# Giving out the product of the attention weights with V two items behind the logits instead of one

## The chip, the cores and the metric

The kernel runs on one core of one Trainium2 chip, in one launch. The metric is device time in microseconds (us); lower is better. Beside the time of each run there is one execution taken by the hardware profiler, from which all rows below come. PE is TensorE (matrix products), PEld its weight loads, DVE is VectorE, ACT ScalarE, POOL GpSimd, SP SyncE.

## The reference, cut to what matters

Everything is fp32. A sequence of 512 tokens of width 1024 passes a first block with three branches (a "fox" attention with forget gates and 12 heads of 64, an S5 state space, a memory attention with 4 heads of 128 over 256 memory rows), then two layers of a second block (attention A with 8 query heads on 2 key heads; attention B with three dilated groups of 4 heads; a wide MLP).

```python
# first block
h = rms_norm(x, g_norm); z = h @ w_in        # q, k, v, forget gates, S5 input, memory q, gates
s = q @ k.T / 8 + F[:, None] - F[None, :]    # fox: F is the cumulated log forget gate, causal
y_fox = softmax(s) @ v * silu(gf)
y_s5 = gelu(s5_ssm(u, ...)); y_s5 = y_s5 * sigmoid(y_s5 @ w_glu + b_glu) * silu(gs)
y_mem = softmax(qm @ mk.T / sqrt(128)) @ mv * silu(gm)
merged = g0 * (y_fox @ w_proj_fox) + g1 * (y_s5 @ w_proj_s5) + g2 * (y_mem @ w_proj_mem)
x = rms_norm(x + merged @ w_out, g_final)
# second block, for each of two layers
h = rms(x, g_mix) * (1 + sc1) + sh1; parts = h @ w_in
y_a = softmax(rope(qa) @ rope(ka).T / 8) @ va @ w_branch_a
y_b = dilated_attention(rope(qs), rope(ks), vs) @ w_branch_b
x = x + gt1 * ((sigmoid(ga) * y_a + sigmoid(gb) * y_b) @ w_out)
x = x + gt2 * (relu(h2 @ w_ff1) ** 2 @ w_ff2)
```

## The kernel before, in words

Each fp32 product is made as three products of rounded halves: a matrix is cast to its high part (`wh`, `ph`, `yh`), the rest is its low part (`wl`, `pl`, `yl`), and PE adds high·high, high·low and low·high in one PSUM tile (lines 117 to 119 and 133 to 135 for the layers' weights). For each strip of weights ACT casts the high part (line 93), and DVE or POOL subtracts it to give the low part (line 96).

All four kinds of attention go through `Att.unit`. There are 16 units: six of fox (two heads each), two of memory, and in each of the two layers two of attention A and two of attention B. A unit has two lists of items. The first list finds each query row's maximum: `s_item` makes logits and reduces them (line 345), and at its end `m_item` splits all maxima in three bf16 parts on DVE (`split3`, lines 267 to 271) and turns them with four products on PE (`turn`, line 277; the split maxima are named mcm, or mcq in attention B). The second list goes over the heads and, within a head, over blocks of keys, 168 items in all (48 of fox, 8 of memory, 56 in each layer). `t_item` makes the logits with keys on the partitions (line 320), ACT takes the exponential (pe, line 388) and rounds it (ph, line 390), DVE subtracts to get pl (line 392). `pv_item` adds the three products with V into the head's PSUM tile ppv (lines 409 to 411: V high·ph, V low·ph, V high·pl). After a head's last one `out_item` copies the sums out (lines 436 and 437), and after a pair's last, in fox, DVE takes the reciprocal (line 439) and POOL multiplies (line 440).

PSUM has three tiles for layer products ("mm"), four in one ring for logits, sums, turns and S5 ("s"), and one for the products with V ("pv").

Items of one unit's second list are dealt among those of the next unit's first list by their relative place (`mix`), and that list among items of projections by counting (`merge`). Each item ends with a tick, which pays the background generators: the S5 batches advance at 0.2, later 0.25, of the ticks during fox and memory. A batch makes s5bt and its product (lines 1259, 1268), copies it (s5b, line 1308), multiplies by weights s5cw (line 1312), copies again (s5to, line 1317) and makes the outputs (lines 1321 to 1323).

None of this is the final order. The program's text gives each instruction a place, and the framework's scheduler then puts the instructions of each engine in an order of its own; buffers, semaphores and waits follow from it. So a shift at one place can reorder every engine anywhere behind it. DVE copies and the normalisation of a row (lines 190, 197, 210, "nr") stand in the same queues.

Of the kernel before, what the change touches and what calls it, by code (L numbers as in the profile page):

```python
# [234 lines left out]
class Att(Core):  # L235

    @staticmethod
    def cut(t, c):  # L240
# [50 lines left out]
    def unit(self, nh, sregs, tregs, qk, vsl, dst, extra=None, nq=4, hd=64, orow=None, fold=None):  # L291
# [82 lines left out]
        def t_item(j, i):  # L374
            if i == 0:
                st["pv", j] = self.p("pv")
            regs, pvs = tregs()[i]
            lo_c = min(c0 for c0, *_ in regs)
            pt = self.p("s")
            w = slice(lo_c, max(c0 + n for c0, n, *_ in regs))  # L380
            qs = w if isinstance(regs[0][3], slice) else regs[0][3]
            own = extra is None and fold is None
            if own:
                nc.tensor.matmul(self.like(pt[:, w], qs), self.selm[j], self.cut(st["mr"], qs), start=True, stop=False)
            for r_i, reg in enumerate(regs):
                region_mm(pt, j, reg, not own and r_i == 0, r_i == len(regs) - 1, True)
            e = self.u(name="pe")
            nc.scalar.activation(out=e[:, w], in_=pt[:, w], func=AF.Exp)  # L388
            ph = self.u(F32R, "ph")
            nc.scalar.copy(ph[:, w], e[:, w])  # L390
            pl = self.u(F32R, "pl")
            nc.vector.tensor_tensor(out=pl[:, w], in0=e[:, w], in1=f32(ph)[:, w], op=ALU.subtract)  # L392
            st["p", j, i] = (ph, pl, pvs)
# [3 lines left out]
        def pv_item(j, i):  # L397
            ph, pl, pvs = st.pop(("p", j, i))
            pv = st["pv", j]
            mm = nc.tensor.matmul  # L400
            for x, (g, kb, c) in enumerate(pvs):
                vh, vl = vsl(j, g, kb)
                o = c
                f = i == 0 and x == 0
                z = i == nt - 1 and x == len(pvs) - 1
                if not isinstance(c, slice):
                    o = slice(0, 4 * (c[1] - c[0]))
                h, lo = self.like(ph[:, o], c), self.like(pl[:, o], c)
                mm(self.cut(pv, c), vh, h, start=f, stop=False)  # L409
                mm(self.cut(pv, c), vl, h, start=False, stop=False)  # L410
                mm(self.cut(pv, c), vh, lo, start=False, stop=z)  # L411
            if i == nt - 1:
                out_item(j)
# [8 lines left out]
        def out_item(j):  # L422
            pv = st.pop(("pv", j))
            v = vrow(j)
            if own_sum:
                rb = self.u(name="rb")
                pb = self.p("m")
                nc.tensor.matmul(pb, self.selr1[j], st["mr"], start=True, stop=True)
                nc.scalar.copy(rb, pb)
                nc.vector.tensor_tensor(out=dst(j), in0=pv, in1=rb, op=ALU.mult)  # L430
                return
            if j % 2 == 0:
                st["rs"] = self.u(name="rs")
            rows = slice(64 * (j % 2), 64 * (j % 2) + 64)
            rs, y = st["rs"], dst(j)
            nc.scalar.copy(rs[rows], pv[64 - v.start:128 - v.start])
            nc.scalar.copy(y[rows], pv[v])
            if j % 2 == 1:
                nc.vector.reciprocal(out=rs, in_=rs)
                nc.gpsimd.tensor_tensor(out=y, in0=y, in1=rs, op=ALU.mult)  # L440
# [3 lines left out]
        seq = [(j, i) for j in range(nh) for i in range(nt)]  # L444
        t = []
        for k, (j, i) in enumerate(seq):
            def it(j=j, i=i, k=k):
                t_item(j, i)
                if k > 0:
                    pv_item(*seq[k - 1])  # L450
            t.append(it)
        t.append(lambda: pv_item(*seq[-1]))
        t = [(lambda f=f: (f(), self.tick(1.0))) for f in t]
        s = [(lambda f=f: (f(), self.tick(0.5))) for f in s]
        return s, t
# [1598 lines left out]
```

## Time and profile before

| | us |
|---|---|
| median of three runs | 2462.0 |
| fastest and slowest of them | 2461.26 and 2466.11 |
| the profiled execution | 2459.34 |
| its span, first to last instruction | 2457.6 |

The profiled execution is 2.7 us under the median and has 1.7 us around its span. The mean clock that was granted to TensorE is 0.981 of full speed in it. Rows give start and duration in us from the span's start; the bracket at a row's end is the time the engine idled before it, and what ended that.

### The profile page before, as it was taken

What the parts mean: (1) busy time and instruction counts of PE and PEld (TensorE: products, weight loads), DVE (VectorE), ACT (ScalarE), POOL (GpSimd) and SP (SyncE); (2) the same over time, 40 slices, a digit from 0 to 9 for tenths busy, and PEclk for the clock granted to TensorE, in tenths of its full rate; (3) what the DMA queues carried; (4) which work ended last, traced back from release to release, by engine and by line L of the source; (5) the groups of instructions that cost most, each with busy time, mean ns of one, the idle gap of its engine ahead of it and who ended that gap; (6) DMA issues with size and microseconds to landing.
All of it is one profiled execution on the core that took longest, in us unless ns stands there. A gap on an engine that the chain in (4) does not pass through costs nothing.

```text
span 2457.6 us, 33152 instructions
## 1 busy us (share of the span) xinstructions
PE 2322.2 (94%) x12138; PEld 1938.8 (79%) x12138; DVE 1538.6 (63%) x2573; ACT 1064.0 (43%) x1995; POOL 887.5 (36%) x810
## 2 busy tenths in 40 slices
PE   6999989989999889998999999998999899999999
PEld 5877768877888767787888888897778788888888
DVE  7567787657899788658278674257874746422222
ACT  4345543443333336643444324343565344533422
POOL 2445446635222264225132223126531523123212
PEclk9999999999999999999999999998999999999999
DMA  4311123312676321122137563232212224223222
GB/s 158 104 44 52 56 75 101 112 43 84 233 270 226 124 83 43 60 77 79 61 129 259 201 217 120 77 138 73 77 36 69 77 69 138 71 101 112 89 92 86
DMA packets 105620, 265.37 MB, mean 108 GB/s; under 512 B 13664, under 2 KB 23408, under 8 KB 105456
## 3 DMA queue, kind: packets, MB, share of 16 engines
q1 hardware_dynamic: 104304, 261.47, 31.5%
q8 instruction: 96, 1.57, 0.3%
q10 hardware_dynamic: 1152, 1.77, 0.2%
q14 instruction: 68, 0.56, 0.1%
HBM read 244.69 MB, written 9.44 MB: 103 GB/s over the span
## 4 chain that ended last, share of the span: by engine, by line
PE 63%; DVE 11%; issue 4%; ACT 3%; POOL 2%; DMA 1%; SPq 1%; DVEq 0%; POOLq 0%; ACTq 0%
PE pmm L117 17%; PE pmm L118 17%; PE pmm L119 17%; PE ps L320 3%; DVE wl L96 1%; DVE adacc L514 1%; DMA xs<-xg 1%; PE ppv L411 1%; PE ppv L410 1%; PE ppv L409 1%; DVE l L232 1%; PE pmm L134 1%; PE pmm L135 1%; PE pmm L133 1%; DVE xs L636 1%
## 5 line engine op out<-in xcount | busy, mean ns | idle before, releaser
L96 POOL TENSOR_TENSOR wl<-wr,wh 128x512 fp32r<-128x512 f32 x346 | 480.8, 1409 | 1122.6 <-ACT wh L93 968.0
L117 PE MATMUL pmm<-h,wh 128*128 128x512 f32 (+1 forms) x2112 | 824.1, 391 | 5.7 <-ACT wh L93 3.2
L119 PE MATMUL pmm<-h,wl 128*128 128x512 f32 (+1 forms) x2112 | 821.2, 389 | 2.1 <-POOL wl L96 1.8
L118 PE MATMUL pmm<-l,wh 128*128 128x512 f32 (+1 forms) x2112 | 819.5, 388 | 0.0
L119 PEld LDWEIGHTS pmm<-h,wl 128*128 128x128 f32 x2112 | 399.1, 189 | 85.7 <-POOL wl L96 4.3
L117 PEld LDWEIGHTS pmm<-h,wh 128*128 128x128 f32 x2112 | 399.4, 189 | 84.7 <-ACT wh L93 4.7
L118 PEld LDWEIGHTS pmm<-l,wh 128*128 128x128 f32 x2112 | 399.6, 189 | 77.3 <-DVE l L230 0.4
L93 ACT CAST wh<-wr 128x512 fp32r<-128x512 f32 (+1 forms) x692 | 385.1, 610 | 136.8 <-DMA wr<-in_w 118.8
L96 DVE TENSOR_TENSOR wl<-wr,wh 128x512 fp32r<-128x512 f32 x346 | 278.8, 836 | 30.3 <-ACT wh L93 26.9
L392 DVE TENSOR_TENSOR pl<-pe,ph 128x512 fp32r<-128x512 f32 (+4 forms) x168 | 121.4, 731 | 149.8 <-ACT ph L390 144.7
L230 DVE TENSOR_TENSOR l<-r,h 128x512 fp32r<-128x512 f32 x64 | 46.5, 726 | 220.9 <-ACT h L222 216.8
L971 DVE SCALAR_TENSOR_TENSOR x<-pmm,ada,x 128x512 f32<-128x512 f32 (+1 forms) x88 | 59.9, 682 | 180.5 <-PE pmm L119 180.0
L320 PE MATMUL ps<-qk,qk 128*128 128x512 f32 (+4 forms) x416 | 142.9, 381 | 24.6 <-POOL qk L683 7.4
L514 DVE SCALAR_TENSOR_TENSOR adacc<-adw,cact,adacc 128x512 f32<-128x512 f32 x168 | 156.5, 932 | 3.2
L994 ACT ACTIVATE r<-pmm 128x512 f32<-128x512 f32 x62 | 37.1, 598 | 257.1 <-PE pmm L119 257.1
L388 ACT ACTIVATE pe<-ps 128x512 f32<-128x512 f32 (+4 forms) x168 | 84.6, 503 | 102.8 <-PE ps L320 102.4
L320 PEld LDWEIGHTS ps<-qk,qk 128*128 128x128 f32 x416 | 81.0, 199 | 51.7 <-POOL qk L683 13.3
L117 PE MATMUL pmm<-yh,wh 128*128 128x512 f32 (+1 forms) x244 | 91.2, 377 | 5.8 <-ACT yh L1419 3.7
L632 POOL TENSOR_TENSOR qv<-qv,mhalf 128x8 f32<-128x8 f32 x34 | 62.9, 1852 | 86.6 <-DVE qv L631 83.1
L119 PE MATMUL pmm<-yh,wl 128*128 128x512 f32 (+1 forms) x244 | 90.7, 373 | 1.7 <-DVE wl L96 0.9
L390 ACT CAST ph<-pe 128x512 fp32r<-128x512 f32 (+4 forms) x168 | 88.8, 529 | 7.8 <-PE ppv L410 1.5
L118 PE MATMUL pmm<-yl,wh 128*128 128x512 f32 (+1 forms) x244 | 90.6, 372 | 0.3 <-DVE yl L1089 0.3
(386 smaller groups left out, 3993.2 us busy)
## 6 DMA issues: line engine op xcount, KB each, us to landing
wr<-in_w SPq DMA_DIRECT2D x324, 512.0 KB
adw<-in_wada SPq DMA_DIRECT2D x192, 256.0 KB
xs<-xg SPq DMA_DIRECT2D x136, 64.0 KB
wr<-in_w SPq DMA_DIRECT2D x22, 384.0 KB
xd<-x SPq DMA_DIRECT2D x16, 256.0 KB
x<-xd SPq DMA_DIRECT2D x16, 256.0 KB
x<-in_x SPq DMA_DIRECT2D x16, 128.0 KB
x<-in_x SPq DMA_DIRECT2D x8, 256.0 KB
```

Of the source, the lines that this page charges most:

```text
L93: ins = self.nc.scalar.copy(h[:, 0:m], r[:, c:c + m])
L96: eng.tensor_tensor(out=l[:, 0:m], in0=r[:, c:c + m], in1=f32(h)[:, 0:m], op=ALU.subtract)
L117: mm(out, wh, ah, start=start, stop=False)
L118: mm(out, wh, al, start=False, stop=False)
L119: self.pe = mm(out, wl, ah, start=False, stop=stop).ins.name
L320: mm(outs[i] if len(r.shape) == 2 else outs[i].rearrange("p (r i) -> p r i", r=r.shape[1]), w, r, start=first and i == 0, stop=last and i ...
L388: nc.scalar.activation(out=e[:, w], in_=pt[:, w], func=AF.Exp)
L390: nc.scalar.copy(ph[:, w], e[:, w])
L392: nc.vector.tensor_tensor(out=pl[:, w], in0=e[:, w], in1=f32(ph)[:, w], op=ALU.subtract)
L514: nc.vector.scalar_tensor_tensor(out=acc, in0=w, scalar=cc, in1=acc, op0=ALU.mult, op1=ALU.add)
L632: nc.gpsimd.tensor_tensor(out=v, in0=v, in1=self.mhalf, op=ALU.pow)
L971: nc.vector.scalar_tensor_tensor(out=x[j][:, s], in0=pm[:, s], scalar=ada[:, c + j:c + j + 1], in1=x[j][:, s], op0=ALU.mult, op1=ALU.add)
```

## The change

Within a unit, the products with V of item k-2 follow the logits of item k, where those of item k-1 did. The last two products of a unit become items of their own, where one did. So a unit's second list has one entry more (and pays one tick more), and the relative places that `mix` and the counts that `merge` deal by shift with its length. No instruction's arithmetic is altered, and each engine has the same work. Lines behind the new one are numbered one higher after the change.

```diff
@@ class Att(Core) @@
+    LAG = 2
@@ def unit(...) @@
         for k, (j, i) in enumerate(seq):
             def it(j=j, i=i, k=k):
                 t_item(j, i)
-                if k > 0:
-                    pv_item(*seq[k - 1])
+                if k >= self.LAG:
+                    pv_item(*seq[k - self.LAG])
             t.append(it)
-        t.append(lambda: pv_item(*seq[-1]))
+        t += [(lambda v=v: pv_item(*v)) for v in seq[len(seq) - self.LAG:]]
         t = [(lambda f=f: (f(), self.tick(1.0))) for f in t]
```

What the built programs' queues show, at three places.

VectorE in layer 0, where the second list of the first attention A unit (pl) and the first list of the next (unm, the reduced maxima) run beside the rotary embedding of the projections to come (xg, xs, rope). Before:

```order
L345 TENSOR_REDUCE unm_2012_8992<-ps_2019_9007 128x1
L345 TENSOR_REDUCE unm_2012_8992<-ps_2024_9022 128x1
L345 TENSOR_REDUCE unm_2012_8992<-ps_2025_9025 128x1
L392 TENSOR_TENSOR pl_2018_9005<-pe_2016_9001,ph_2017_9003 128x512
L647 TENSOR_TENSOR xg_1952_8725<-xg_1952_8725,ps_2032_9063 128x512
L392 TENSOR_TENSOR pl_2023_9017<-pe_2021_9013,ph_2022_9015 128x512
L636 TENSOR_TENSOR xs_2010_8984<-xs_2010_8984,rope_1814_7987 128x512
```

and after:

```order
L346 TENSOR_REDUCE unm_2012_8992<-ps_2019_9007 128x1
L346 TENSOR_REDUCE unm_2012_8992<-ps_2024_9019 128x1
L393 TENSOR_TENSOR pl_2018_9005<-pe_2016_9001,ph_2017_9003 128x512
L346 TENSOR_REDUCE unm_2012_8992<-ps_2029_9034 128x1
L637 TENSOR_TENSOR xs_2010_8984<-xs_2010_8984,rope_1814_7987 128x512
L648 TENSOR_TENSOR xg_1952_8725<-xg_1952_8725,ps_2036_9072 128x512
L393 TENSOR_TENSOR pl_2023_9017<-pe_2021_9013,ph_2022_9015 128x512
```

The second pl stood ahead of xs and now stands behind xs and xg.

VectorE at the turn of the fifth fox unit's maxima: the CASTs and subtractions of mcm0 and sp3 are the split in three, on which PE's turn waits; qk belongs to a projection, s5to to an S5 batch, wl to layer weights. Before:

```order
L345 TENSOR_REDUCE unm_550_2548<-ps_599_2722 128x1
L96 TENSOR_TENSOR wl_586_2656<-wr_475_2154,wh_585_2655 128x512
L345 TENSOR_REDUCE unm_550_2548<-ps_600_2727 128x1
L670 SCALAR_TENSOR_TENSOR qk_589_2686<-pmm_588_2661,qk_589_2686 64x512
L267 CAST mcm0_6_74<-unm_550_2548 128x4x4
L268 TENSOR_TENSOR sp3_605_2746<-unm_550_2548,mcm0_6_74 128x16
L269 CAST mcm0_6_74<-sp3_605_2746 128x4x4
L325 MEMSET unm_1092_4897 128x16
L270 TENSOR_TENSOR sp3_605_2746<-sp3_605_2746,mcm0_6_74 128x16
L1086 TENSOR_TENSOR s5cw_577_2641<-s5w_579_2643,s5w_580_2644 64x16x16
L670 SCALAR_TENSOR_TENSOR qk_590_2689<-pmm_588_2661,qk_590_2689 64x512
```

and after (four s5to copies, of which three are shown):

```order
L346 TENSOR_REDUCE unm_554_2560<-ps_607_2759 128x1
L393 TENSOR_TENSOR pl_604_2750<-pe_602_2746,ph_603_2748 128x384
L268 CAST mcm0_6_74<-unm_554_2560 128x4x4
L269 TENSOR_TENSOR sp3_612_2778<-unm_554_2560,mcm0_6_74 128x16
L1318 COPY s5to_599_2730<-ps_598_2721 32x512
...
L1318 COPY s5to_599_2730<-ps_598_2721 32x4x64
L1318 COPY s5to_599_2730<-ps_598_2721 32x4x32
L270 CAST mcm0_6_74<-sp3_612_2778 128x4x4
L326 MEMSET unm_1096_4909 128x16
L393 TENSOR_TENSOR pl_611_2773<-pe_609_2769,ph_610_2771 128x256
L271 TENSOR_TENSOR sp3_612_2778<-sp3_612_2778,mcm0_6_74 128x16
L272 CAST mcm0_6_74<-sp3_612_2778 128x4x4
```

Four copies of the S5 batch now stand between the first steps of the split. On PE, between the unit's last logits for maxima and this turn, stood 31 products, 24 of them of layer weights, and now stand 20, none of layer weights.

PE at the end of the last fox unit: ppv is the head's sum, pmm with h, l, wh and wl a projection, L1312 and L1321 to L1323 an S5 batch (one line higher after), L190 and L197 a normalisation, and yh the gated result going into the next projection. Before:

```order
L409 MATMUL ppv_768_3445<-ph_809_3601,v_482_2217 128x128
L410 MATMUL ppv_768_3445<-ph_809_3601,v_484_2221 128x128
L411 MATMUL ppv_768_3445<-pl_810_3603,v_482_2217 128x128
L119 MATMUL pmm_826_3683<-h_41_182,wl_797_3538 128x512
...
L117 MATMUL pmm_826_3683<-h_48_189,wh_798_3541 128x512
L118 MATMUL pmm_826_3683<-l_56_197,wh_798_3541 128x512
L119 MATMUL pmm_826_3683<-h_48_189,wl_799_3542 128x512
L1312 MATMUL ps_819_3651<-s5cw_790_3527,s5b0_818_3645 32x128
...
L1323 MATMUL ps_828_3710<-s5m_726_3279,s5cw_791_3528 128x128
L190 MATMUL ps_847_3773<-c32_2_67,sacc_731_3291 128x1 x4
L197 MATMUL ps_850_3782<-c32_2_67,nr_849_3780 128x128 x2
L117 MATMUL pmm_858_3801<-yh_834_3743,wh_811_3608 128x512
```

and after:

```order
L119 MATMUL pmm_832_3715<-h_48_189,wl_803_3559 128x512
L410 MATMUL ppv_772_3454<-ph_812_3619,v_482_2214 128x128
L411 MATMUL ppv_772_3454<-ph_812_3619,v_484_2218 128x128
L1322 MATMUL ps_821_3666<-u4_120_499,s5to_809_3606 128x128
L1323 MATMUL ps_821_3666<-s5m_711_3203,s5cw_784_3506 128x128
L1324 MATMUL ps_821_3666<-s5m_713_3205,s5cw_785_3507 128x128
...
L1324 MATMUL ps_821_3666<-s5m_713_3205,s5cw_785_3507 128x128
L412 MATMUL ppv_772_3454<-pl_813_3621,v_482_2214 128x128
L190 MATMUL ps_849_3780<-c32_2_67,sacc_731_3291 128x1 x4
L197 MATMUL ps_852_3789<-c32_2_67,nr_851_3787 128x128 x2
L117 MATMUL pmm_860_3808<-yh_836_3750,wh_814_3629 128x512
```

48 products stood between the last product with V and the first with yh (a row with x4 or x2 holds four or two); the 6 of lines 190 and 197 stand there now, and the 12 S5 products stand ahead of the last product with V.

## Rows read from the trace of the kernel before

**Rows 1.** The page, first lines: span, then busy time, share and instructions per engine

```profile
span 2457.6 us, 33152 instructions
...
PE 2322.2 (94%) x12138; PEld 1938.8 (79%) x12138; DVE 1538.6 (63%) x2573; ACT 1064.0 (43%) x1995; POOL 887.5 (36%) x810
```

**Rows 2.** The page's chain that ended last, share of the span by engine

```profile
PE 63%; DVE 11%; issue 4%; ACT 3%; POOL 2%; DMA 1%; SPq 1%; DVEq 0%; POOLq 0%; ACTq 0%
```

**Rows 3.** Waits of PE: waiter <- releaser: us in total, times, longest

```profile
PE ps L277 <- DVE mcq L271: 20.5, 4, 6.4
...
PE ps L320 <- ACT pe L388: 5.4, 5, 2.2
...
PE ppv L411 <- DVE pl L392: 3.5, 5, 1.6
...
PE ppv L409 <- ACT ph L390: 0.9, 1, 0.9
```

**Rows 4.** Line 392: count, ns min/median/max, first and last start, forms

```profile
L392 DVE TENSOR_TENSOR pl<-pe,ph x168: 260/685/1814, 122.7 to 2026.2; 128x512 fp32r<-128x512 f32 x100, 128x256 fp32r<-128x256 f32 x28, 128x192 fp32r<-128x192 f32 x16, 128x384 fp32r<-128x384 f32 x12
```

**Rows 5.** Layer 1 from 1752 us: start, us, instruction [idle before <-releaser]

```profile
1752.48 1.75 DVE L636 TENSOR_TENSOR xs<-xs,rope 128x512 f32<-128x512 f32 x1
...
1753.65 3.40 POOL L96 TENSOR_TENSOR wl<-wr,wh 128x512 fp32r<-128x512 f32 x2
...
1754.16 1.75 DVE L392 TENSOR_TENSOR pl<-pe,ph 128x512 fp32r<-128x512 f32 x1
...
1755.96 0.50 PE L411 MATMUL ppv<-pl,v 128*128 128x512 f32 x1 [1.64 <-DVE pl L392]
```

**Rows 6.** Window after it: us, PE, PEld, DVE, ACT, POOL busy, PEclk, DMA, GB/s

```profile
1757.00:1767.00 10.00, 9.16 (x50) 7.59 (x48) 9.66 (x19) 3.21 (x7) 6.72 (x8) 0.83 0.25 79
```

**Rows 7.** Layer 0 at the same place

```profile
934.26 0.68 DVE L392 TENSOR_TENSOR pl<-pe,ph 128x512 fp32r<-128x512 f32 x1
```

**Rows 8.** End of the sixth fox unit, time in order

```profile
340.15 0.28 PE L411 MATMUL ppv<-pl,v 128*128 128x128 f32 x1
...
340.58 0.58 ACT L436 COPY rs<-ppv 64x512 f32<-64x512 f32 x1
...
343.75 3.35 DVE L439 RECIPROCAL rs<-rs 128x512 f32<-128x512 f32 x1
...
348.48 1.51 DVE L1086 TENSOR_TENSOR yf<-gt,yf 128x512 f32<-128x512 f32 x1 [1.38 <-POOL yf L440]
...
349.91 1.96 DVE L1317 COPY s5to<-ps 32x512 f32<-32x512 f32 x4
...
352.02 0.77 PE L1321 MATMUL ps<-u,s5to 128*128 128x128 f32 x2 [4.65 <-DVE s5to L1317]
...
357.90 1.04 DVE L1086 TENSOR_TENSOR gw<-gw,s5y 128x512 f32<-128x512 f32 x1
...
358.49 0.97 PE L197 MATMUL ps<-c,nr 128*128 128x128 f32 x4 [1.17 <-POOL nr L210]
...
360.71 0.63 ACT L1419 ACTIVATE yh<-gw 128x512 fp32r<-128x512 f32 x1 [1.11 <-DVE gw L1089]
...
361.92 1.22 PE L117 MATMUL pmm<-yh,wh 128*128 128x512 f32 x2 [2.45 <-ACT yh L1419]
```

**Rows 9.** Turn of the third fox unit, memory attention's start and end: PE

```profile
186.05 0.40 PE L277 MATMUL ps<-c,mcm 128*128 128x128 bf16 x4 [1.45 <-DVE mcm L271]
...
497.74 0.40 PE L277 MATMUL ps<-c,mcm 128*128 128x128 bf16 x4 [2.07 <-DVE mcm L271]
...
550.53 2.05 PE L1268 MATMUL ps<-u,s5bt 128*128 128x128 f32 x16 [1.62 <-ACT s5bt L1259]
...
563.25 0.72 PE L117 MATMUL pmm<-yh,wh 128*128 128x512 f32 x2 [1.30 <-ACT yh L1419]
```

**Rows 10.** PE's waits in two S5 batches of the background

```profile
425.04 2.05 PE L1312 MATMUL ps<-s5cw,s5b 128*32 128x128 f32 x16 [1.83 <-DVE s5b L1308]
...
588.96 0.38 PE L1312 MATMUL ps<-s5cw,s5b 128*32 128x128 f32 x2 [3.00 <-DVE s5b L1308]
```

## The prediction, on record before the run

> **What bounds the kernel now.** I read the page first. PE is busy 2322.2 of 2457.6 us, 94%, and no other engine passes 63% [rows 1]; in the chain that ended last 63% is PE and 11% VectorE [rows 2]. So time can come only out of PE's gaps, 2457.6 - 2322.2 = 135 us, and out of stretches in which its clock is low. The list of PE's waits says whose they are [rows 3]. The waits that the change speaks of are few: PE stood 3.5 us in five places for pl and 0.9 us in one for ph, 4.4 us over 168 items [rows 3, 4]. Far larger is the turn of attention B's maxima, 20.5 us in four places, in which no weight is multiplied with V, and which the change doesn't touch. Line 392 is the operation that the product waits for: 168 subtractions, median 0.685 us, up to 1.814 [rows 4].
>
> Then I read the built queues, since the text's order isn't the order that runs. I counted the rows of PE between an item's last logits product and its first product that reads pl: the median over the 168 items is 36 before and 40 after; in fox's 48 items 28.5 and 29. Thus the scheduler already holds the products with V far behind their logits, which is why so few wait, and the extra distance in the text becomes four rows. What the change does beyond that is to deal everything around the units anew, since each second list is one entry longer. So I cost it place by place.
>
> **The direct effect.** The 4.4 us of waits for ph and pl [rows 3] is all that a longer distance can give; nothing is the other end, since waits of this kind arise where a subtraction stands late on VectorE, not where rows are missing on PE. The distance grows by 4 of 36 rows, a ninth, so I am nearer to nothing, and take a fifth of the 4.4: -0.9 (ends -4.4 and 0).
>
> **Layer 0's second pl.** After the change xs and xg stand ahead of it on VectorE. The trace of before has that order in layer 1: xs takes 1.75 us, pl behind it 1.75, and PE then waits 1.64 [rows 5]. The clock granted in the 10 us behind is 0.83 [rows 6], between the levels 1.2 and 2.4 GHz after that gap, which costs 10 x 0.17 = 1.7 us. In layer 0 pl took 0.68 [rows 7]. Layer 0 should now look like layer 1: 1.64 + 1.7 = +3.3 (ends 0, if other products cover it, and +3.3).
>
> A row's length matters here: pl's 1.75 us in layer 1 lie beside POOL's weight subtractions, 3.40 us from 1753.65 [rows 5]; in layer 0 it took 0.68. The Trainium skill (SBUF — State Buffer, "Who interferes with whom") explains that a VectorE instruction with two SBUF inputs and a GpSimd one that reads SBUF keep each other out of a shared port. By that rule alone, with POOL idle at layer 0's place, pl would be 1.75 - 0.68 = 1.1 us earlier, the wait 0.5 instead of 1.64, and the sum 1.1 us less. The trace agrees with that rule as far as these two lengths go.
>
> **The fifth fox unit's turn.** Its split in three on VectorE gets the four s5to copies into the middle, 1.96 us by the like ones at the sixth unit's end [rows 8], and on PE the 24 weight products that ran meanwhile, at the page's mean of 2322.2/12138 = 0.19 us 4.6 us of work [rows 1], stand elsewhere. The third fox unit's turn had only 4 rows of PE between the last logits and itself, and there PE waited 1.45; memory's first, with 36, waited 2.07 [rows 9]. With the copies in it a bare turn is 2.07 + 1.96 = 4.0 at most. But 20 rows of logits and S5 are left as cover, 3.8 us at the mean, and against 4 x 0.19 + 1.45 + 1.96 = 4.2 us of the third unit's split with copies that leaves 0.4. I take +1.0 (ends 0 and +4.0), since rows of fox's logits are shorter than the mean.
>
> **The end of the sixth fox unit.** Before, PE waited 4.65 for s5to, 1.17 for nr and 2.45 for yh [rows 8], 8.27 in sum, while the last product with V was long done. After, the S5 products come before that product, so the 4.65 goes; but then the whole chain from the last product to yh stands bare: the product 0.28, two copies of 0.58 on ACT (one stands), the reciprocal 3.35, a gw operation of 1.04, yf 1.51, a second gw of 1.04, and yh twice 0.63, since gw's cast stands in ACT's queue ahead of the one that the first product reads [rows 8]: 0.28 + 1.16 + 3.35 + 1.04 + 1.51 + 1.04 + 1.26 = 9.6. PE has lines 190 and 197 in it, about 1 us (0.97 for the latter) [rows 8]. 8.6 to 9.6 of gap instead of 8.27, with small instructions in the chain not counted: +1.0 (ends 0 and +1.9).
>
> **S5's batches.** Between a batch's product of line 1268 and that of line 1312 stood 139 rows of PE in the third and 131 in the fifth, and PE waited 1.83 and 3.00 us at two such places [rows 10]; now there are 154 and 152. 15 and 21 rows more at 0.19 us are 2.9 and 4.0 us of cover, more than the waits: -4.8 (ends -4.8 and 0).
>
> **Memory.** At its end stood 1.62 for s5bt and 1.30 for yh [rows 9]. Line 1268 now stands 22 instead of 12 rows behind its transposes, and 19 rows instead of 1 stand ahead of the yh product: 10 and 18 rows at 0.19 are 1.9 and 3.4 us: -2.9 (ends -2.9 and 0). At its start an S5 product of line 1312 now comes two products after the turn where 29 stood, with two s5cw products on VectorE inside the split. That is the kind of place which cost 3.00 [rows 10]: +3.0 (ends 0 and 3.0 + 2.07 = +5, if the turn [rows 9] lengthens by as much again).
>
> **The sum.** -0.9 + 3.3 + 1.0 + 1.0 - 4.8 - 2.9 + 3.0 = -0.3. The profiled execution's 2459.34 becomes 2459.0; the median of the runs lies 2.7 higher at 2462.0, so 2461.7, call it 2462. The ends add up to -12.1 and +14.2: 2450 to 2476.
>
> **The rivals.** *Slower: the turns of fox.* Between the last maxima logits and the turn stood 31, 31 and 55 rows on PE in the fourth, fifth and sixth unit, and now 15, 20 and 22. If VectorE's last reduction and split take longer than that cover, 2.9 us for 15 rows at 0.19, each of the three stands bare like the third's 1.45 [rows 9], with a low-clock stretch behind as after layer 1's gap, 1.7 [rows 6]: 3 x 3.15 = 9.5 in place of the fifth's 1.0, so +8.2, 2470. For it: memory's first turn had 36 rows and waited 2.07 all the same [rows 9], because its split was late on VectorE. Against: the third unit's split was over 4 rows and 1.45 after its logits [rows 9], some 2.2 us, under 2.9.
>
> *Faster: the distance does what it says.* Layer 1's wait goes with its low clock, as do the other waits for ph and pl (-4.4 - 1.7), layer 0 keeps its order in time, the fifth turn is covered, and S5, memory and the fox end go as in the sum: -6.1 - 4.8 - 2.9 + 1.0 + 3.0 = -9.8, 2452. For it: VectorE is busy only 63% [rows 1], and four more rows of PE, 0.8 us, are half of layer 1's 1.64 [rows 5]. Against: pl there was late by VectorE's queue, and the queue in layer 0 now becomes the same.
>
> *Slower: the ring of PSUM tiles.* Logits two items ahead of the products take tiles from the "s" ring earlier; PE waited 5.4 us for exponentials to free one [rows 3]. Should that double, -0.3 + 5.4 gives 2467. Against: a tile is freed by the exponential, not by the product with V, so the distance itself holds none. The Trainium skill (Perfetto Trace Analysis, "Optimization Strategy") says that a gap that repeats on the engine to be kept busy can mean too little PSUM for the next tile; here the gap repeats only five times, so the trace bears it out little.
>
> *It doesn't do what it says* is not a rival but part of the forecast: 36 rows become 40.
>
> **How the numbers follow.** A measurement of this kernel can tell about 0.2%, 4.9 us, from no change: 2457 to 2467. The forecast's case holds 0.45 and has that as its own range; the faster case, at 2452, 0.28; the turns 0.18; the ring 0.09. The range goes to the bounds of the sum, 2450 to 2476, and leaves out some 0.1 at either end. Faster 0.28, same 0.45, slower 0.27.
>
> **What would show it.** Right: in layer 0 at about 936 us a wait of some 1.6 us for pl ahead of line 412, and the granted clock under 0.9 behind it; at about 352 us no wait for s5to, and a single one of 8 to 9 us for yh at the fox end; S5's waits of 1.83 and 3.00 gone; PE's busy time within a few us of 2322.2 and its total of gaps near 135. Wrong: waits of 2 us or more for mcm at three fox turns (slower), a sum of gaps under 128 (faster), or waits for exponentials of 10 us in sum (the ring). Since the order is dealt anew everywhere, a gap at a place that I didn't read is what would most likely make it wrong.

## The result and the profile after

The changed kernel takes 2476.45 us (median of four runs, 2474.24 to 2478.02), the kernel before 2462.89 beside it: a ratio of 1.0053, interval 1.0035 to 1.0070, 13.6 us slower. 2462 and "no change" had been forecast, and 2476.45 lies just above the range's end of 2476. The profiled execution took 2477.86 us, 18.5 more than that of before, so it shows some 5 us more than the medians do.

The first lines of the page of after:

```profile
span 2476.1 us, 33169 instructions
...
PE 2325.8 (94%) x12138; PEld 1943.7 (78%) x12138; DVE 1539.8 (62%) x2573; ACT 1064.4 (43%) x1995; POOL 887.3 (36%) x810
...
PE 72%; DVE 13%; issue 6%; ACT 4%; POOL 4%; DMA 1%; SPq 0%; DVEq 0%; POOLq 0%; ACTq 0%
```

The work is the same [rows 1]; PE's gaps grow from 135 to 2476.1 - 2325.8 = 150 us, and its busy time by 3.6. The chain's shares [rows 2] say little here: the kernel below with S5's rate lowered, as fast as before, has 72% PE and 13% VectorE in it too. In the list of PE's waits those that the change speaks of hardly move (pl 3.7 us in six places, against 3.5 in five [rows 3]), nor does attention B's turn:

```profile
PE ps L278 <- DVE mcq L272: 23.4, 5, 6.4
...
PE ps L197 <- POOL nr L210: 9.9, 6, 6.1
...
PE ps L321 <- ACT pe L389: 3.8, 3, 2.8
PE ppv L412 <- DVE pl L393: 3.7, 6, 1.7
```

To see where the time went I cut both executions at the same products: where the front ends, at fox's end (first product with yh), and at the start of layer 0. The view of windows for before, fox and then the rest of the first block (columns as in [rows 6]):

```profile
33.99:361.92 327.93, 304.96 (x1719) 251.58 (x1719) 231.42 (x451) 156.10 (x297) 150.44 (x172) 0.95 0.22 72
361.92:813.31 451.39, 427.73 (x2157) 357.10 (x2157) 346.31 (x517) 175.72 (x339) 186.54 (x161) 0.98 0.43 148
```

and for after:

```profile
34.86:374.28 339.42, 305.89 (x1719) 252.42 (x1719) 232.00 (x451) 157.15 (x297) 150.84 (x172) 0.95 0.21 68
374.28:834.41 460.13, 434.14 (x2156) 360.90 (x2157) 349.18 (x516) 174.84 (x339) 186.41 (x162) 0.97 0.43 146
```

Fox is 11.5 us longer with the same 1719 products, of which 0.9 is busy time and 10.6 waiting. The rest of the first block is 8.7 longer, of which 6.4 is busy time at a granted clock of 0.97 instead of 0.98, and 2.3 waiting. The front is 0.9 longer, and the two layers together 2.6 shorter. So all of the loss is made in the two stretches beside which the S5 batches run, and none in the layers, where 112 of the 168 items are.

Apart from a wait of 6.15 at fox's end, which comes up below, the two largest new waits have one form. In fox, PE's rows and then VectorE's, of after:

```profile
328.60 0.22 PE L321 MATMUL ps<-c 128*128 128x128 bf16 x1
332.49 0.67 PE L119 MATMUL pmm<-h,wl 128*128 128x512 f32 x1 [3.67 <-DVE wl L96]
...
327.17 4.68 DVE L1285 TENSOR_TENSOR_SCAN s5g<-s5keep,s5m 128x128 f32<-128x128 f32 x8
331.77 2.34 DVE L96 TENSOR_TENSOR wl<-wr,wh 128x512 fp32r<-128x512 f32 x2
```

Eight scans of an S5 batch stand on VectorE ahead of the low parts of weights, and PE waits 3.67 us for these. In the kernel before, the same scans took as long, but the two subtractions stood ahead of them, and PE waited for low parts from VectorE at this line only once, 0.9 us (first two rows of VectorE, then PE's waits before and after):

```profile
318.00 1.29 DVE L96 TENSOR_TENSOR wl<-wr,wh 128x512 fp32r<-128x512 f32 x2
319.21 4.73 DVE L1284 TENSOR_TENSOR_SCAN s5g<-s5keep,s5m 128x128 f32<-128x128 f32 x8
...
PE pmm L119 <- DVE wl L96: 0.9, 1, 0.9
...
PE pmm L119 <- DVE wl L96: 5.8, 4, 3.7
```

The 3.67 is about a third of the 10.6 us by which PE waits longer in fox. The end of fox adds 0.6; the rest lies in waits of 2.3 us and less, which no run took apart. In the memory stretch:

```profile
591.63 3.79 DVE L1087 TENSOR_TENSOR s5cw<-s5w,s5w 64x256 f32<-64x256 f32 x4 [1.00 <-POOL s5cw L1223]
...
592.02 2.68 POOL L96 TENSOR_TENSOR wl<-wr,wh 128x512 fp32r<-128x512 f32 x2
...
595.45 0.69 DVE L1090 SCALAR_TENSOR_TENSOR gl<-gl,pmm 128x512 f32<-128x512 f32 x1
...
596.28 0.77 PE L117 MATMUL pmm<-h,wh 128*128 128x512 f32 x1 [3.57 <-DVE gl L1090]
...
596.30:606.30 10.00, 10.00 (x38) 7.99 (x39) 2.84 (x7) 1.39 (x2) 0.33 (x1) 0.70 0.11 43
```

Four S5 multiplications stand ahead of the gate gl, which empties a PSUM tile; PE waits 3.57 for that tile and then works 10 us at a granted clock of 0.70, between the levels 1.2 and 2.4 GHz, some 3 us (10 x 0.30) more than at full clock. The same four of this batch took 1.72 before:

```profile
584.70 1.72 DVE L1086 TENSOR_TENSOR s5cw<-s5w,s5w 64x256 f32<-64x256 f32 x4 [5.32 <-POOL s5cw L1222]
```

The Trainium skill (SBUF — State Buffer, "Who interferes with whom") has a VectorE instruction with two SBUF inputs contend with a GpSimd one that reads SBUF; the trace agrees, in that 2.68 us of weight subtractions on POOL lie inside the 3.79. But not all of this wait is loss: before, PE waited 3.00 [rows 10] and 0.73 us for s5b in this batch, and the 10 us behind that had a clock of 0.83. The 3.57 takes the place of these, and by these numbers what is left is about 1 us, from the clock.

### The profile page after: what moved, and what is told of

Its sections match the earlier page's. It is cut to its first block, busy times and chain, and to the rows that moved or that the text cites. A ratio compares the mean times of both kernels' runs of the same rounds, so it can differ in the third digit from the quotient of the medians.

```text
span 2476.1 us, 33169 instructions
## 1 busy us (share of the span) xinstructions
PE 2325.8 (94%) x12138; PEld 1943.7 (78%) x12138; DVE 1539.8 (62%) x2573; ACT 1064.4 (43%) x1995; POOL 887.3 (36%) x810
## 4 chain that ended last, share of the span: by engine, by line
PE 72%; DVE 13%; issue 6%; ACT 4%; POOL 4%; DMA 1%; SPq 0%; DVEq 0%; POOLq 0%; ACTq 0%
PE pmm L119 19%; PE pmm L117 19%; PE pmm L118 19%; PE ps L321 4%; DVE wl L96 1%; PE ppv L412 1%; PE ppv L410 1%; PE ppv L411 1%; DVE adacc L515 1%; PE pmm L134 1%; PE pmm L135 1%; PE pmm L133 1%; DMA xs<-xg 1%; DVE unm L346 1%; POOL wl L96 1%
## 5 line engine op out<-in xcount | busy, mean ns | idle before, releaser
L96 DVE TENSOR_TENSOR wl<-wr,wh 128x512 fp32r<-128x512 f32 x346 | 268.9, 807 | 39.8 <-ACT wh L93 36.5
L393 DVE TENSOR_TENSOR pl<-pe,ph 128x512 fp32r<-128x512 f32 (+4 forms) x168 | 111.9, 672 | 140.6 <-ACT ph L391 131.9
L515 DVE SCALAR_TENSOR_TENSOR adacc<-adw,cact,adacc 128x512 f32<-128x512 f32 x168 | 150.2, 895 | 3.3
```

The lines of the kernel that those rows point to most:

```text
L96: eng.tensor_tensor(out=l[:, 0:m], in0=r[:, c:c + m], in1=f32(h)[:, 0:m], op=ALU.subtract)
L515: nc.vector.scalar_tensor_tensor(out=acc, in0=w, scalar=cc, in1=acc, op0=ALU.mult, op1=ALU.add)
```

## The experiments

All times are medians in us; each ratio is against runs of the kernel before on the same chip and has its interval behind it. The kernel before was at 2461.22 for the first four, 2460.92 for the next four, 2462.25 from S5-behind to the split scans, and 2460.78 for the last four.

### Which units

Distance two in one kind of unit, one in the others; the condition is `extra is not None` for fox, `own_sum` for memory, neither of them for the layers:

```diff
         own_sum = hd == 128
+        lag = self.LAG if extra is not None else 1
-                if k >= self.LAG:
-                    pv_item(*seq[k - self.LAG])
+                if k >= lag:
+                    pv_item(*seq[k - lag])
-        t += [(lambda v=v: pv_item(*v)) for v in seq[len(seq) - self.LAG:]]
+        t += [(lambda v=v: pv_item(*v)) for v in seq[len(seq) - lag:]]
```

Fox alone:

> The longer distance in the six fox units alone; memory and layers keep one item. Between the same two products PE needed 327.9 us for fox before and 339.4 after. If the loss is made in fox, this kernel is 9 to 13 us slower than before (2472 to 2476). If the loss came with memory's part of the change (rival), it is within 4 us of before.

Measured 2475.26, 1.0057 (1.0042 to 1.0072), 14.0 slower: the loss comes with fox's part. Memory alone:

> The longer distance in the two memory units alone. Memory's stretch, with the S5 batches behind it, took 318.5 us before and 326.0 after. If memory's own lists make that, this is 5 to 8 us slower than before (2468 to 2471). If those 7.5 us are inherited from fox, whose S5 batches arrive at another point, it is within 4 us of before.

Measured 2461.12, 1.0003 (0.9993 to 1.0012): none. So the 8.7 of the rest of the first block is inherited from fox, or needs both. The layers alone:

> The longer distance in the eight units of the two layers alone. The layers took 0.8 and 1.8 us less after than before, so 2 to 3 us faster than before (2460) if nothing else acts; 3 us or more slower if layer 0's second pl behind xs costs what the prediction said.

Measured 2462.35, 1.0003 (0.9993 to 1.0012). Neither case: the layers' part does nothing that can be measured.

### Which part of the change

The change has three: the distance, one more entry in each list (dealing), and one more tick in each list, which advances the S5 batches by 0.2 of it. Distance one, with an empty entry that ticks:

```diff
-    LAG = 2
+    LAG = 1
         t += [(lambda v=v: pv_item(*v)) for v in seq[len(seq) - self.LAG:]]
+        t.append(lambda: None)
```

> The distance stays at one item; each unit's second list gets one empty entry at its end, so that the dealing and the ticks are those of the changed kernel. If the longer list (dealing and S5's extra tick) makes the loss, 10 to 15 us slower than before (2473 to 2478). If the distance itself makes it, within 4 us of before.

Measured 2475.09, 1.0060 (1.0045 to 1.0075). Without any longer distance the loss is all there. The distance without the longer list:

```diff
-        t += [(lambda v=v: pv_item(*v)) for v in seq[len(seq) - self.LAG:]]
+        t.append(lambda: [pv_item(*v) for v in seq[len(seq) - self.LAG:]])
```

> The distance of two items, but a unit's last two products with V stay in one entry, so that a second list is as long as before and pays as many ticks. If the longer list makes the loss, within 4 us of before (2457 to 2465). If the distance adds to it by itself, 9 to 15 us slower.

Measured 2468.48, 1.0030 (1.0019 to 1.0042), 7.6 slower, between the two. Its profiled execution took 2461.86, the fastest of its runs, so the trace can't show where the others lost; this stays open. The changed kernel with the extra entry's tick left out:

```diff
-        t = [(lambda f=f: (f(), self.tick(1.0))) for f in t]
+        t = [(lambda f=f, n=n: (f(), self.tick(1.0) if n < len(seq) + 1 else None)) for n, f in enumerate(t)]
```

> The changed kernel, but a list's extra entry pays no tick, so that the S5 batches stand against the items as before, with the dealing shifted. If S5's advance by the extra tick makes the loss, within 4 us of before. If the dealing makes it, 10 to 15 us slower as the changed kernel.

Measured 2458.32, 0.9989 (0.9980 to 0.9999): the loss is gone, and this is the fastest kernel with distance two. The tick alone, distance and list as before:

```diff
+    LAG = 1
-        t = [(lambda f=f: (f(), self.tick(1.0))) for f in t]
+        t = [(lambda f=f, n=n: (f(), self.tick(1.0 if n < len(seq) else 2.0))) for n, f in enumerate(t)]
```

> Before, with the last entry of each second list paying two ticks: the S5 advance alone, with neither distance nor dealing. If the extra tick makes the loss, 10 to 15 us slower than before; if the dealing, within 4 us.

Measured 2478.58, 1.0072 (1.0057 to 1.0087), 17.7 slower, even a little over the 15 expected. The dealing alone:

```diff
+    LAG = 1
         t += [(lambda v=v: pv_item(*v)) for v in seq[len(seq) - self.LAG:]]
+        t.append(None)
-        t = [(lambda f=f: (f(), self.tick(1.0))) for f in t]
+        t = [(lambda f=f: (f(), self.tick(1.0)) if f else None) for f in t]
```

> Before, with an empty entry without a tick at the end of each second list: the dealing alone. If the dealing makes the loss, 10 to 15 us slower than before; if the extra tick, within 4 us. If both this and the extra tick alone cost 5 us or more, then any shift costs, and the order before is a favourable one among its neighbours.

Measured 2459.35, 0.9995 (0.9986 to 1.0004): nothing. This kernel and the one without the tick differ in the distance alone, 2459.35 against 2458.32, so beside the longer list the distance is worth 1.0 us, too little to be told from nothing. Beside the old list, with no tick added, it cost 7.6, and why isn't shown.

The collision in fox goes with the tick. In the runs of fox alone, of the empty entry and of the tick alone the eight scans stand ahead of the two weight subtractions, as in the changed kernel, and PE waits 3.67, 3.79 and 4.19 us there. In the kernel without the tick and in that with the dealing alone the subtractions stand ahead, as before, and there is no such wait.

### S5's standing

S5 behind by what the change puts it ahead:

```diff
+    LAG = 1
-        t = [(lambda f=f: (f(), self.tick(1.0))) for f in t]
+        t = [(lambda f=f, n=n: (f(), self.tick(1.0) if n < len(seq) else None)) for n, f in enumerate(t)]
```

> Before, with the last entry of each second list paying no tick: S5's batches fall behind by the amount by which the changed kernel puts them ahead. If S5 standing early is what costs, within 4 us of before or faster. If any other place of S5 against the attention items costs (the order before being a favourable one), 8 us or more slower.

Measured 2474.94, 1.0053 (1.0038 to 1.0068). The other way costs as much. For the next ones S5's generator gets a start, 1.2 here:

```diff
+    LAG = 1
         self.s5 = self.add_bg(self.s5_gen(u, self.y5, ge, ges), self.RS5)
+        self.s5[1] = 1.2
```

> Before, with S5's generator started 1.2 ahead, which is what the six fox units' extra ticks add up to (6 x 1.0 x 0.2), and no extra tick. If what costs is S5's standing at the end of fox and in memory, 10 to 16 us slower. If it is the way there (an extra tick at each unit's end), within 4 us of before.

Measured 2475.28, 1.0054 (1.0039 to 1.0069), with no list, distance or tick changed. Here one wait stands out, with ScalarE in the middle; rows of this kernel:

```profile
273.14 3.35 DVE L440 RECIPROCAL rs<-rs 128x512 f32<-128x512 f32 x1
...
273.26 0.63 ACT L1683 ACTIVATE gw<-gw 128x512 f32<-128x512 f32 x1 [0.37 <-DVE gw L1087]
...
276.40 0.95 DVE L1090 SCALAR_TENSOR_TENSOR gw<-gw,s5y 128x512 f32<-128x512 f32 x1
...
277.38 0.63 ACT L1420 ACTIVATE yh<-gw 128x512 fp32r<-128x512 f32 x1 [3.49 <-DVE gw L1090]
277.92 1.12 ACT L93 CAST wh<-wr 128x512 fp32r<-128x512 f32 x2
...
278.57 0.80 PE L117 MATMUL pmm<-h,wh 128*128 128x512 f32 x1 [7.18 <-ACT wh L93]
```

S5's gw stands on VectorE behind a fox unit's reciprocal, ScalarE's yh waits for gw, the cast of weights is queued behind yh, and PE waits 7.18 us for weights that had nothing to do with either. Some 2.5 us of it are the reciprocal's: ScalarE was done with gw at 273.89, and VectorE came to it at 276.40. The rest is gw's own way over the two engines, behind which the cast stands. The changed kernel with S5's rate lowered so that it arrives at fox's end about as before:

```diff
-    RS5, RS5B, RADA = 0.2, 0.25, 0.37
+    RS5, RS5B, RADA = 0.1957, 0.25, 0.37
```

> The changed kernel with S5's rate at 0.1957 instead of 0.2, so that by the end of fox S5 is about where it was before. If S5's standing costs, most of the 14 us comes back: 2458 to 2466. If the extra ticks cost by something else, 2472 to 2479.

Measured 2459.65, 0.9994 (0.9984 to 1.0003): all of it comes back with one number, distance and longer list kept. Then the size of the shift, as above with -0.6, 0.4 and 2.4 in place of 1.2:

> Before, with S5's generator started 0.6 behind (half of what the extra ticks shift), distance and lists as before. If time depends on S5's standing smoothly, with the best at before's standing, 3 to 7 us slower (2465 to 2469). If it is a matter of single steps that fall into another item (no rule of size), it can be anywhere from 3 us faster to 15 slower.

Measured 2471.97, 1.0053 (1.0038 to 1.0068), 11.2 slower.

> Before, with S5 started 0.4 ahead. If time depends on the standing smoothly, 2 to 5 us slower (2464 to 2467). If by single steps, anywhere from 3 us faster to 15 slower, and not between before and the start 1.2 ahead.

Measured 2459.27, 0.9996 (0.9987 to 1.0006), no change.

> Before, with S5 started 2.4 ahead, twice the shift of the extra ticks. If the loss grows with the shift, 20 us slower or more; if it is a matter of which items the steps fall to, 5 to 18 us slower as at half the shift, or none.

Measured 2494.59, 1.0142 (1.0127 to 1.0157), 33.8 slower. Neither expectation holds throughout: -0.6 costs more and 0.4 less than a smooth course would, but 2.4 costs more than single steps were to. Over these five starts (-0.6, 0, 0.4, 1.2, 2.4) it looks like a valley, flat from 0 to 0.4 and higher on both sides; in between nothing was measured. Behind, the loss hardly grows: S5 behind by 1.2 at fox's end, the run above without the last ticks, cost 12.7 against 11.2. Where the time goes differs by side. Windows of S5 0.6 behind, fox and then the rest of the first block:

```profile
33.68:360.71 327.03, 304.63 (x1718) 250.93 (x1719) 226.46 (x450) 156.69 (x298) 150.16 (x172) 0.96 0.21 71
360.71:829.05 468.34, 435.66 (x2159) 361.84 (x2158) 355.95 (x518) 175.39 (x337) 186.10 (x161) 0.97 0.41 143
```

and of S5 1.2 ahead:

```profile
34.17:374.84 340.67, 304.82 (x1718) 250.96 (x1719) 229.29 (x451) 156.57 (x297) 152.15 (x172) 0.94 0.21 68
374.84:828.46 453.62, 430.50 (x2156) 359.64 (x2157) 351.55 (x516) 175.44 (x339) 186.48 (x162) 0.97 0.43 148
```

Behind, fox is as before and the second stretch 17 us longer (the layers are 3 shorter in that profile); ahead, fox is 13 longer and the second 2 (2.4 ahead pays for both: 341.0 and 472.4). The changed kernel, at 339.4 and 460.1, is of the kind that is ahead. The last one is the changed kernel without the extra tick, started 1.2 ahead:

> The distance of two with no tick for the extra entry, which by itself was 2 to 3 us faster than before, and S5 started 1.2 ahead. If the loss belongs to S5's standing whatever the distance is, 10 to 16 us slower than before. If the two act on each other, within 5 us.

Measured 2488.72, 1.0117 (1.0100 to 1.0133), 27.9 slower. Beyond both cases: S5's standing costs whatever the distance, but 1.2 ahead costs 13.0 with the distance of one and 27.9 + 2.6 = 30.5 with two. The parts don't add up.

### One of the collisions

The changed kernel with the scans in two steps, so that the weights can pass between:

```diff
             g.append(o)
-        yield 1.6
+            yield 0.8
```

> The changed kernel with S5's eight scans given out as two steps of four, which lets VectorE take the two weight subtractions between them at the place where PE waited 3.67 us at 332 us. The same S5 budget. If that collision is a part of the loss, the wait falls to about 1.3 us and the kernel is 2 to 5 us faster than the changed one, 2470 to 2474. If the wait only moves, 2474 to 2479.

Measured 2482.43, 1.0086 (1.0071 to 1.0101), 20.2 slower than before, where the changed kernel was 13.6. At the place itself, VectorE's rows and then PE's (the view ends before the last scan):

```profile
325.89 1.36 DVE L1285 TENSOR_TENSOR_SCAN s5g<-s5keep,s5m 128x128 f32<-128x128 f32 x4
327.18 1.26 DVE L96 TENSOR_TENSOR wl<-wr,wh 128x512 fp32r<-128x512 f32 x2
328.36 3.16 DVE L1285 TENSOR_TENSOR_SCAN s5g<-s5keep,s5m 128x128 f32<-128x128 f32 x3
...
327.89 0.51 PE L119 MATMUL pmm<-h,wl 128*128 128x512 f32 x1 [0.74 <-DVE wl L96]
```

The wait falls from 3.67 to 0.74, even under the expected 1.3, and fox, cut at the same products, takes 334.9 us instead of 339.4: the collision is part of fox's loss. But the kernel as a whole is slower than the changed one, outside both expected ranges; in its one profile layer 1 is 5.5 longer. Why stays open, and no run shows that removing the collision makes the kernel faster.

## Why the prediction was wrong

The step that failed is the sum, which goes "place by place" and has no term for the extra tick: it puts the tick at nothing without a reason, though the description of the change says that each list pays one more, and it has S5's part as a gain, "-4.8". That tick moves S5 against the attention items, and the runs show that it alone costs 17.7 us, all of the 13.6 and more, while dealing (1.6 gained) and, beside the longer list, distance (1.0 gained) are next to nothing. The last sentence, on a gap "at a place that I didn't read", named the risk but gave it no size. That 2476.45 lies so near the range's end of 2476 is luck: that end was made of layer 0's +3.3, the fifth turn's +4.0, the fox end's +1.9 and memory's +5, and of these only the fox end's came.

Point by point. **The direct effect**, -0.9: 1.0 gained beside the longer list, too little to be told from nothing, and 7.6 lost beside the old one, so the term is not confirmed. The waits for pl and ph came to 4.6 us, where they were 4.4 [rows 3]. **Layer 0's second pl**, +3.3: no. It stands behind xs and xg as the queue said, but took 1.19 and PE waited 0.28, and the clock granted behind it was 1.00, so the 1.7 for a low clock didn't come either (the last row is a window, with columns as in [rows 6]):

```profile
955.18 0.69 DVE L637 TENSOR_TENSOR xs<-xs,rope 128x512 f32<-128x512 f32 x1
955.79 0.68 DVE L648 TENSOR_TENSOR xg<-xg,ps 128x512 f32<-128x512 f32 x1
956.38 1.19 DVE L393 TENSOR_TENSOR pl<-pe,ph 128x512 fp32r<-128x512 f32 x1
...
957.63 0.50 PE L412 MATMUL ppv<-pl,v 128*128 128x512 f32 x1 [0.28 <-DVE pl L393]
...
955.23 1.80 POOL L636 TENSOR_TENSOR xg<-xg,rope 128x512 f32<-128x512 f32 x1 [5.97 <-DMA xs<-xg]
...
957.00:967.00 10.00, 7.58 (x44) 5.47 (x42) 9.84 (x16) 6.76 (x13) 8.40 (x9) 1.00 0.27 80
```

The xs that had taken 1.75 in layer 1 [rows 5] took 0.69 here. An order shows who stands ahead, not how long it takes: both 1.75s of before lay beside work on POOL, and I had priced them as if they belonged to the order. POOL worked beside xs here too. In layer 1 of before its xg had begun 0.09 us ahead of xs; here it began 0.05 behind, and it was POOL's that took longer:

```profile
1752.39 1.30 POOL L635 TENSOR_TENSOR xg<-xg,rope 128x512 f32<-128x512 f32 x1 [6.20 <-PE ps L629]
```

The sentence on the shared port gave 0.5 for this wait, nearer than the 1.64 that went into the sum, but it supposed POOL idle here, and it wasn't. Layer 1's own wait went as well, to 0.34.

**The fifth fox unit's turn**, +1.0: no wait at 308.48, 0. **The end of fox**, +1.0: the 4.65 for s5to went and the bare chain came, as the steps said:

```profile
364.01 3.35 DVE L440 RECIPROCAL rs<-rs 128x512 f32<-128x512 f32 x1
...
368.79 1.51 POOL L210 TENSOR_TENSOR nr<-nv,mhalf 128x2 f32<-128x2 f32 x1
...
370.35 1.22 PE L197 MATMUL ps<-c,nr 128*128 128x128 f32 x4 [6.15 <-POOL nr L210]
...
374.28 1.22 PE L117 MATMUL pmm<-yh,wh 128*128 128x512 f32 x2 [2.71 <-ACT yh L1420]
...
376.83 0.80 PE L118 MATMUL pmm<-yl,wh 128*128 128x512 f32 x1 [1.33 <-DVE yl L1090]
```

6.15 + 2.71 = 8.9 for the 8.27 [rows 8], +0.6, and with the 1.33 behind it +1.9; the reciprocal holds nv on VectorE, and POOL's yf holds nr, so that PE stood mostly for nr and not for yh. The chain was right, and so was its size. **S5's batches**, -4.8: both waits went [rows 10], and those for s5b fell from 5.6 to 1.4 us in sum, near what was forecast. But waits for s5bw, another tile of the batches, make 4.1 where there were none, and s5cw and the scans now meet the gate and the weights, 3.57 and 3.67, so S5's part as a whole is no gain. **Memory**, -2.9 and +3.0: the wait for yh at its end is 1.30 as before, and one of 2.09 for s5bw took the place of the 1.62 for s5bt; the turn's 2.07 is gone at its start, and no wait for line 1313 came there.

Of the rivals, the turns of fox did not come, nor did the ring: waits for the exponentials fell from 5.4 to 3.8 us. The faster case's -6.1 for ph and pl did not come either.

What is shown is that S5's standing against the attention items sets the loss, both ways, and that undoing the shift undoes it beside the longer list. Collisions of S5 with other work on VectorE are seen at three places (3.67, 3.57 and, with the start of 1.2, 7.18 us); only the first follows the tick through the runs, and that such collisions make all of the loss is only argued. The 7.6 of the distance beside the old list and the 30.5 of distance and start together stay open.

## What to carry to other kernels

When an edit lengthens a list from which a background stream is paced, it moves the stream, and that can outweigh the edit's purpose: test the edit with the pace held fixed before judging it, and in more than one way, for held in two ways here it came out 2.6 us faster and 7.6 slower. Put a size on all that is dealt anew: here kernels with equal work lay between 2458 and 2495. And from a queue's order read who stands ahead, never how long it takes.

## What the runs showed that was not expected

Starting S5 2.4 ahead, with nothing else changed, costs 33.8 us, 1.4%; 0.4 ahead costs nothing. But 0.6 behind costs 11.2, so somewhere within 0.6 behind the kernel before a loss begins. And a wait for plain weights of 7.18 us can be lengthened, here by some 2.5, by a reciprocal on VectorE, by way of another instruction in ScalarE's queue.
